# Three value panels of a streaming encoder: products in halves of 256 columns, each activation part used twice in a row, or in row halves of the array into four banks

## The chip, the cores and the metric

The kernel runs on one core of a Trainium2 chip. Its engines are TensorE (PE in the profile, with its weight loads shown apart as PEld), VectorE (DVE), ScalarE (ACT), GpSimd (POOL) and SyncE (SP), which issues the transfers. The metric is the device time in microseconds (us); lower is better. Times of a kernel are medians of several runs.

## The reference, cut to what matters

The reference computes a two-layer encoder trunk over 256 positions and a model width of 2048, all in float32. The change lies in the first mixer, and only in the product that makes its values.

```python
u = rms_norm(h, a_norm_g[l])
proj = u @ a_w_in[l]                      # (256 x 2048) @ (2048 x (3*2048 + 16))
q, k, v, fz = jnp.split(proj, [D, 2 * D, 3 * D], axis=-1)
...
v = v.reshape(B, S, H, Dh)                # 16 heads of 128
...
o = forgetting_attention(q, k, v, logf)
h = h + o.reshape(B, S, D) @ a_w_out[l]
...
```

After it come a squared-ReLU MLP, one shared key and value projection, a second mixer with chunked attention, and a second MLP.

## The kernel before, in words

**Three passes stand for one float32 product.** Every weight tile and every activation is split into a high part, rounded to fp32r, and a low part, the rest. A product is then high x high, low activation x high weight, high activation x low weight. ScalarE makes the high weights (line 210, tile `hi`), VectorE the low ones (line 211, tile `lo`), for a unit of 128 x 1024 weights at a time. `fetch` keeps up to three units ready; `hi` and `lo` have three buffers each, so that the `hi` of a unit needs the buffer of three units before.

**A panel** (`panels`) is 512 output columns. It runs over 8 units of two blocks of 128 rows each (`UA` = 2). In a unit, `products` issues 12 matmuls of 512 columns: two row blocks times two blocks of 128 positions (`NB` = 2) times three passes. `passes` holds the lines of the passes: 444 for high x high, 446 for low activation x high weight, 448 for high activation x low weight. The stationary operand is the activation (128 x 128), the moving one the weights. The sums of a panel stand in a pair of PSUM banks, one for each block of positions, and `acc_pair` deals out two such pairs in turn.

**The order of the work.** The first mixer goes over four groups of four heads. A group has three panels: queries, keys, values. At the end of a key panel, `head_norm` squares the sums, and its last step `turn` (line 529, tile `qn`) reads the bank of each block of positions once more. That step isn't done at once: it goes into a list, `fill`, of which `run_fill` does one entry after each unit. So the key banks of block 0 are read after unit 0 of the value panel, those of block 1 after its unit 1. The attention of a group (`attend`: scores on lines 582 and 583, values times probabilities on lines 614 and 615) is spread in the same way over the units that follow. At the end of a value panel `v_evac` (line 639) scales both banks into SBUF on ScalarE. After the fourth group comes `stage` with the output projection, whose first call runs two panels side by side and takes both pairs of banks.

**The written order holds** on VectorE, ScalarE, TensorE and SyncE: the last line of the kernel fixes it (`keep_order`). Each engine takes its instructions in that order and stands still at the first that has to wait.

Of the kernel before, what the change touches and what calls it, by code (L numbers as in the profile page):

```python
# [9 lines left out]
F32 = mybir.dt.float32  # L10
F32R = mybir.dt.float32r
AF = mybir.ActivationFunctionType
ALU = mybir.AluOpType
AX = mybir.AxisListType

P = 128
T = 256
NB = T // P
D = 2048
KT = D // P  # L20
# [10 lines left out]
UA = UN // 512  # L31
# [16 lines left out]
def trunk(ctx: ExitStack, tc: tile.TileContext, xT, xr, gs, hg, bf, wgate, w_in, w_oa, w1a, w2fa, w2sa,  # L48
          w_kv, w_qb, w_ob, w1b, w2fb, w2sb, rel, out):
    nc = tc.nc  # L50
    V, S, G, TE, SY = nc.vector, nc.scalar, nc.gpsimd, nc.tensor, nc.sync

    def pool(name, bufs, **kw):
        return ctx.enter_context(tc.tile_pool(name=name, bufs=bufs, **kw))
# [6 lines left out]
    wk = pool("wk", 6)  # L61
# [30 lines left out]
    first = sm.tile([P, GH], F32, name="first", bufs=1)  # L92
# [7 lines left out]
    units = deque()  # L100
# [79 lines left out]
    ready = deque()  # L180
# [39 lines left out]
    def fetch(ahead=AHEAD, early=EARLY):  # L220
        while (units or raws) and sum(1 for r in ready if not r[2]) <= ahead and not (half_next() and any(r[2] for r in ready)):
            issue()
        while units and sum(1 for r in raws if r[1]) < early:
            load()
        return ready.popleft()[:2]
# [3 lines left out]
    def run_fill():  # L229
        if fill:  # L230
            for f in fill.popleft():
                f()
# [7 lines left out]
    def acc_pair(which=None):  # L240
        if which is None:
            which, turns[0] = turns[0], 1 - turns[0]
        if which == 2:
            return [ps_s.tile([P, 512], F32, name="s") for _ in range(2)]
        return [ps_acc.tile([P, 512], F32, name="acc", tag=f"acc{which}{b}", bufs=1) for b in range(NB)]
# [37 lines left out]
    def room(tag, name, dtype=F32):  # L283
        return qkv.tile([P, WIDE], dtype, name=name, tag=tag, bufs=1 if tag == "bias" else 2)
# [17 lines left out]
    def steps(make):  # L302
        box = []

        def step():
            if not box:
                box.append(make())
            next(box[0])
        return step
# [24 lines left out]
    def turned(name=None):  # L334
        z = qkv.tile([P, GH * T], F32, name="z")
        return (z, qkv.tile([P, GH * T], F32, name=name, tag=name, bufs=2)) if name else z
# [101 lines left out]
    def passes(items, hi, lo, **kw):  # L438

        def cut(w, j):  # L440
            return w[:, j * 512 : (j + 1) * 512]

        for ps, (xh, _), j, first, _ in items:
            TE.matmul(ps, xh, cut(hi, j), start=first, stop=False, **kw)  # L444
        for ps, (_, xl), j, _, _ in items:
            TE.matmul(ps, xl, cut(hi, j), start=False, stop=False, **kw)  # L446
        for ps, (xh, _), j, _, last in items:
            TE.matmul(ps, xh, cut(lo, j), start=False, stop=last, **kw)  # L448

    def products(ps, hi, lo, x, u, halves=False, fast=None, apart=False):  # L450
        kw = {"skip_group_check": True} if fast else {}

        def item(j, b):
            k = u * UA + j if fast is None or u > 1 else 2 * j + u
            return ps[b], [x[k][:, i, b * P : (b + 1) * P] for i in range(2)], j, k == 0 and not fast, k == KT - 1

        J, B = range(UA), range(NB)
        if apart:
            groups = [[(j, b) for b in B] for j in J]
        elif halves:  # L460
            groups = [[(j, b) for j in J] for b in B]
        else:
            groups = [[(j, b) for b in B for j in J]]
        for g in groups:
            passes([item(*i) for i in g], hi, lo, **kw)
# [10 lines left out]
            items.append((ps[i not in (4, 5)][i in (1, 5)], xp, g % 2, i < 2 and g == 0, i < 2 and g == stop))  # L476
        passes(items, hi, lo, skip_group_check=True)

    def panels(x, evacs, before=None, after=None, which=(None, None), tail=None):
        ps = [acc_pair(i) for i in which[: len(evacs)]]  # L480
        for u in range(KT // UA - (3 if tail else 0)):
            if before:
                before(u)
            for q, evac in enumerate(evacs):
                hi, lo = fetch(min(u // 2, AHEAD), 2) if before else fetch()
                products(ps[q], hi, lo, x, u, not units and not ready, apart=bool(before) and u < 2)
                run_fill()
                if u == KT // UA - 1:
                    for b in range(NB):
                        evac(b, ps[q][b])  # L490
                if after:
                    after()
        if tail:
            tail.x, tail.ps, tail.evac = x, ps, evacs
# [12 lines left out]
    def head_norm(stats, z, dst, late=0, apart=None):  # L507

        rest = []

        def f(b, ps):
            sq = wk.tile([P, 512], F32, name="sq", tag="wk")
            ss = sm.tile([P, GH], F32, name="ss")
            rn = sm.tile([P, GH], F32, name="rn")

            def square():
                S.activation(sq, ps, AF.Square)

            def total():
                V.tensor_reduce(ss, sq.rearrange("p (a d) -> p a d", a=GH), axis=AX.X, op=ALU.add)  # L520

            def norm():
                vv = sm.tile([P, GH], F32, name="vv")
                V.tensor_scalar(vv, ss, 1.0 / P, stats().e[:, b : b + 1], op0=ALU.mult, op1=ALU.add)  # L524
                G.tensor_tensor(rn, vv, mhalf, op=ALU.pow)  # L525

            def turn():
                qn = wk.tile([P, 512], F32, name="qn", tag="wk")
                V.tensor_tensor(qn.rearrange("p (a d) -> p a d", a=GH), ps.rearrange("p (a d) -> p a d", a=GH),
                                rn.unsqueeze(2).to_broadcast([P, GH, P]), op=ALU.mult)  # L530
                blocks32(qn, z, b)

            if apart is None:
                square()
            rest.append((square, total, norm, turn))
            if b == NB - 1:
                turns = [[t] for _, _, _, t in rest] + carry(z, dst)
                if apart is not None:
                    add_fill([[]] * apart + [[s, t, n] for s, t, n, _ in rest] + turns)
                    return  # L540
                for _, total, norm, _ in rest:
                    total()
                    if not late:
                        norm()
                add_fill([[]] * (late - 1) + ([[n for _, _, n, _ in rest]] if late else []) + turns)
        return f

    def scale_q(land, layer, g):
        tag = "qs"[g // 2]
        q = qkv.tile([P, GH, T], F32, name="q", tag=tag, bufs=2)  # L550
        S.activation(q.rearrange("p a (b i c) -> p (a b) i c", b=NB, i=4),
                     land.rearrange("p (i ab c) -> p ab i c", i=4, c=32), AF.Copy, scale=gqk[:, layer : layer + 1])
        return q
# [83 lines left out]
    def v_evac(v, r):  # L637
        def f(b, ps):
            S.activation(v[:, b, :], ps, AF.Copy, scale=r[:, b : b + 1])
        return f  # L640

    def add_fill(items):
        for i, it in enumerate(items):
            if i < len(fill):
                fill[i] = fill[i] + it
            else:
                fill.append(it)


    st0 = RowStats("x")  # L650
    x = []
# [16 lines left out]
    def rows_in(i):  # L668
        b, n = chunks[i]
        c = slice(n * 512, (n + 1) * 512)  # L670
        SY.dma_start(h[b][:, c], xr[b][:, c])
# [86 lines left out]
    for g in range(NG):  # L758
        zq, lq = turned("z")
        qb = {}  # L760
        late = 6 if g == 0 else 0
        panels(x, [head_norm(lambda: st0, zq, lq, late)], begin if g == 0 else None)
        if g == 0:
            step = steps(head_gains)
            add_fill([[step], [], [], [], [step]])
            add_fill([[lambda i=i: rows_in(i)] for i in range(5, 8)])
            add_fill([[lambda i=i: st0.add(*chunks[i])] for i in range(3, 8)])
            fill[4].insert(len(fill[4]), st0.roots)
            add_fill(gates(x, st0))
        add_fill([[]] * (7 + late) + [[lambda qb=qb, lq=lq, g=g: qb.update(q=scale_q(lq, 0, g))]])  # L770
        zk, k = turned(), room("k", "k")[:, : GH * T]
        v = room("v", "v")[:, :UN].rearrange("p (b c) -> p b c", b=NB)
        panels(x, [head_norm(lambda: st0, zk, k)])
        add_fill(attend(g, lambda qb=qb: qb["q"], k, v, lambda: ct["cq"], o, decay_bias))
        panels(x, [v_evac(v, st0.r)])

    def bring(p, name):
        p.t[name] = room("kv"[name in ("12", "21")], "w" + name)
# [146 lines left out]
    for g in range(NG):  # L925
        zk, k = turned(), room("k", "k")[:, : GH * T]
        v = room("v", "v")[:, :UN].rearrange("p (b c) -> p b c", b=NB)
# [85 lines left out]
```

## Time and profile before

| | |
|---|---|
| median of 3 runs | 2124.96 us (2121.89 to 2129.16) |
| span of the profiled execution | 2124.3 us |
| TensorE busy | 2101.3 us (99%), 9278 matmuls |
| weight loads busy | 1729.3 us (81%) |
| VectorE busy | 1654.6 us (78%) |
| ScalarE busy | 1211.3 us (57%) |
| value panels of groups 1, 2, 3 end at | 149.9, 220.6, 291.3 us |

The span goes from the first to the last instruction of one execution; no time of its own is listed for that execution, and the median of the runs lies 0.7 us above its span. The ends of the panels are the starts of the first `v_evac` of each. In the timeline a row is a run of like instructions: start, length of the run, engine, line, operation, tiles, count, and in brackets how long the engine stood idle before it and what ended that. A run of matmuls is longer than the distance to the next one, since one ends after the next has begun.

### The profile page before, as it was taken

Reading aid. Unit: us, or ns where it says so; the run is one execution under the profiler, and the core shown is the slowest. Engines: PE = TensorE matmul, PEld = TensorE weight load, DVE = VectorE, ACT = ScalarE, POOL = GpSimd, SP = SyncE. Lnnn points to the kernel's source line nnn. Section 1 sums busy time; section 2 is a strip of 40 time slices with the busy share of each in tenths; the row PEclk is TensorE's granted clock in tenths of the full one; section 3 lists DMA queues with packets and bytes.
Section 4 is the critical chain, followed back from the end, with each engine's and each line's share of the span. In section 5 each row is a group of like instructions: output and inputs, shape, how many; then the busy total and the mean of one; then the engine's idle time right before and its main releaser. Section 6 shows DMA issues by size and latency. Waiting matters only on the chain.

```text
span 2124.3 us, 26113 instructions
## 1 busy us (share of the span) xinstructions
PE 2101.3 (99%) x9278; PEld 1729.3 (81%) x9278; DVE 1654.6 (78%) x1931; ACT 1211.3 (57%) x1519; POOL 49.1 (2%) x48
## 2 busy tenths in 40 slices
PE   9999999999999999999999999999999999999999
PEld 7888888877888887888788888888788878878887
DVE  5767776888788878878877677678887887888786
ACT  6544445665566566556575454456654655665664
POOL 1001000000000000000001010000000000000000
PEclk9999999999999999999999999999999999999999
DMA  8787788776676576477577777787766766765763
GB/s 281 244 249 243 224 264 255 238 246 210 220 256 206 200 265 228 170 239 269 181 240 261 234 228 235 239 276 237 247 211 217 241 203 222 248 212 195 261 234 129
DMA packets 179283, 491.63 MB, mean 231 GB/s; under 512 B 36416, under 2 KB 73424, under 8 KB 179152
## 3 DMA queue, kind: packets, MB, share of 16 engines
q1 hardware_dynamic: 179152, 489.96, 69.8%
q8 instruction: 73, 1.20, 0.2%
q14 instruction: 58, 0.48, 0.1%
HBM read 450.01 MB, written 39.87 MB: 231 GB/s over the span
## 4 chain that ended last, share of the span: by engine, by line
PE 84%; DVE 7%; DMA 4%; ACT 2%; issue 2%; SPq 1%; ACTq 0%; DVEq 0%
PE acc L446 23%; PE acc L448 23%; PE acc L444 23%; PE s L444 4%; PE s L446 4%; PE s L448 4%; DVE lo L211 3%; ACT hi L210 2%; DVE w L790 1%; DVE loh L211 1%; DMA q<-turn 1%; DMA turn<-z 1%; DMA raw<-in_w_in 1%; DVE wT L790 1%; PE s L583 1%
## 5 line engine op out<-in xcount | busy, mean ns | idle before, releaser
L211 DVE TENSOR_TENSOR lo<-raw,hi 128x1024 fp32r<-128x1024 f32 (+1 forms) x610 | 738.2, 1215 | 260.1 <-ACT hi L210 253.0
L210 ACT ACTIVATE hi<-raw 128x1024 fp32r<-128x1024 f32 (+1 forms) x610 | 640.8, 1053 | 367.3 <-PE acc L446 266.8
L444 PE MATMUL acc<-hi,act 128*128 128x512 f32 x2208 | 608.4, 394 | 2.0 <-ACT hi L210 1.1
L446 PE MATMUL acc<-hi,act 128*128 128x512 f32 x2208 | 599.7, 390 | 6.4 <-DVE act L814 6.4
L448 PE MATMUL acc<-lo,act 128*128 128x512 f32 x2208 | 598.4, 390 | 0.0
L446 PEld LDWEIGHTS acc<-hi,act 128*128 128x128 f32 x2208 | 413.4, 188 | 98.2 <-DVE act L814 10.7
L448 PEld LDWEIGHTS acc<-lo,act 128*128 128x128 f32 x2208 | 413.3, 188 | 89.0 <-DVE lo L211 3.2
L444 PEld LDWEIGHTS acc<-hi,act 128*128 128x128 f32 x2208 | 412.9, 188 | 87.9 <-ACT hi L210 2.1
L210 ACT ACTIVATE hi<-w 128x1024 fp32r<-128x1024 f32 x160 | 169.1, 1057 | 226.4 <-DVE w L790 105.2
L211 DVE TENSOR_TENSOR lo<-w,hi 128x1024 fp32r<-128x1024 f32 x160 | 194.8, 1218 | 83.9 <-ACT hi L210 83.8
L444 PE MATMUL s<-hi,act 128*128 128x512 f32 x416 | 112.6, 389 | 0.0
L446 PE MATMUL s<-hi,act 128*128 128x512 f32 x416 | 112.5, 389 | 0.0
L448 PE MATMUL s<-lo,act 128*128 128x512 f32 x416 | 112.5, 389 | 0.0
L210 ACT ACTIVATE hi<-wT 128x1024 fp32r<-128x1024 f32 x64 | 67.7, 1057 | 54.9 <-DVE wT L790 27.9
L448 PEld LDWEIGHTS s<-lo,act 128*128 128x128 f32 x416 | 78.1, 188 | 16.2
L446 PEld LDWEIGHTS s<-hi,act 128*128 128x128 f32 x416 | 78.1, 188 | 16.2
L444 PEld LDWEIGHTS s<-hi,act 128*128 128x128 f32 x416 | 78.0, 188 | 16.2
L211 DVE TENSOR_TENSOR lo<-wT,hi 128x1024 fp32r<-128x1024 f32 x64 | 78.2, 1222 | 9.4 <-ACT hi L210 7.5
L210 ACT ACTIVATE hih<-w 128x512 fp32r<-128x512 f32 x80 | 49.8, 622 | 24.2 <-PE acc L446 16.0
L617 ACT ACTIVATE act<-po 128x256 fp32r<-128x256 f32 x32 | 12.3, 384 | 86.0 <-PE po L615 86.0
L211 DVE TENSOR_TENSOR loh<-w,hih 128x512 fp32r<-128x512 f32 x80 | 54.8, 685 | 7.3 <-ACT hih L210 7.3
L525 POOL TENSOR_TENSOR rn<-vv,mhalf 128x4 f32<-128x4 f32 x32 | 43.3, 1366 | 385.0 <-DVE vv L524 384.9
(190 smaller groups left out, 1717.0 us busy)
## 6 DMA issues: line engine op xcount, KB each, us to landing
raw<-in_w1a SPq DMA_DIRECT2D x96, 512.0 KB, 4.4
raw<-in_w1b SPq DMA_DIRECT2D x96, 512.0 KB, 4.5
raw<-in_w_in SPq DMA_DIRECT2D x94, 512.0 KB, 4.6
raw<-in_w2sa SPq DMA_DIRECT2D x80, 512.0 KB, 4.3
raw<-in_w2sb SPq DMA_DIRECT2D x80, 512.0 KB, 4.2
raw<-in_w_kv SPq DMA_DIRECT2D x64, 512.0 KB, 4.6
turn<-z SPq DMA_DIRECT2D x60, 512.0 KB, 4.2
w<-in_w2fa SPq DMA_DIRECT2D x32, 768.0 KB, 7.6
```

The lines of the kernel that those rows point to most:

```text
L210: S.activation(hi[:, c], raw[:, c], AF.Copy)
L211: V.tensor_tensor(lo[:, c], raw[:, c], hi[:, c].bitcast(F32), op=ALU.subtract)
L444: TE.matmul(ps, xh, cut(hi, j), start=first, stop=False, **kw)
L446: TE.matmul(ps, xl, cut(hi, j), start=False, stop=False, **kw)
L448: TE.matmul(ps, xh, cut(lo, j), start=False, stop=last, **kw)
L525: G.tensor_tensor(rn, vv, mhalf, op=ALU.pow)
L583: TE.matmul(s[:, P : 3 * P], q[:, a, P:T], k[:, a], start=True, stop=True)
L617: S.activation(o[i][:, 0], po[:, :T], AF.Copy)
L790: V.tensor_tensor(d, a, b, op=op)
```

## The change

The value panels of groups 1, 2 and 3 are given another way of doing units 1 to 6; units 0 and 7 and all other panels stay as they were.

- Group 1, `short_halves`: each matmul of 512 columns becomes two of 256, with the same stationary operand. There are 144 instead of 72.
- Group 2, `repeats`: the three products of a block are issued together: the high activation with high weights, the same high activation with low weights, the low activation with high weights. The number stays 72.
- Group 3, `row_halves`: each matmul over 128 rows becomes two over 64 rows, the lower half and the upper half of the array. The second half adds up in a second pair of banks, which the panel takes with a second call of `acc_pair`. There are 144 of 512 columns. At the end ScalarE copies each bank of the second pair to SBUF, VectorE adds it into the first pair, and `v_evac` follows.

```diff
+    def row_halves(k, b, ps, xs, w, first, last):
+        for i in range(2):
+            c = slice(64 * i, 64 * i + 64)
+            TE.matmul(ps[2 * i + b], xs[c], w[c], start=first and i == 1, stop=last and i == 1, skip_group_check=True)
+
+    def short_halves(k, b, ps, xs, w, first, last):
+        for i in range(2):
+            c = slice(256 * i, 256 * i + 256)
+            TE.matmul(ps[b][:, c], xs, w[:, c], start=False, stop=False, skip_group_check=True)
+
+    def repeats(ps, hi, lo, x, u):
+        for j in range(UA):
+            k, c = u * UA + j, slice(j * 512, (j + 1) * 512)
+            for b in range(NB):
+                xh, xl = (x[k][:, i, b * P : (b + 1) * P] for i in range(2))
+                for xs, w in ((xh, hi), (xh, lo), (xl, hi)):
+                    TE.matmul(ps[b], xs, w[:, c], start=False, stop=False, skip_group_check=True)
+
+    def split_products(how, ps, hi, lo, x, u):
+        if how is repeats:
+            repeats(ps, hi, lo, x, u)
+            return
+        for i, w in ((0, hi), (1, hi), (0, lo)):
+            for j in range(UA):
+                k = u * UA + j
+                for b in range(NB):
+                    how(k, b, ps, x[k][:, i, b * P : (b + 1) * P], w[:, j * 512 : (j + 1) * 512],
+                        k == UA and not i and w is hi, k == KT - UA - 1 and w is lo)
+
...
-    def panels(x, evacs, before=None, after=None, which=(None, None), tail=None):
+    def panels(x, evacs, before=None, after=None, which=(None, None), tail=None, how=None):
         ps = [acc_pair(i) for i in which[: len(evacs)]]
+        if how is row_halves:
+            ps[0] += acc_pair()
...
-                products(ps[q], hi, lo, x, u, not units and not ready, apart=bool(before) and u < 2)
+                if how and 0 < u < KT // UA - 1:
+                    split_products(how, ps[q], hi, lo, x, u)
+                else:
+                    products(ps[q], hi, lo, x, u, not units and not ready, apart=bool(before) and u < 2)
                 run_fill()
                 if u == KT // UA - 1:
                     for b in range(NB):
+                        if how is row_halves:
+                            both = wk.tile([P, 512], F32, name="both", tag="wk")
+                            S.activation(both, ps[q][2 + b], AF.Copy)
+                            V.tensor_tensor(ps[q][b], ps[q][b], both, op=ALU.add)
                         evac(b, ps[q][b])
...
-        panels(x, [v_evac(v, st0.r)])
+        panels(x, [v_evac(v, st0.r)], how=(None, short_halves, repeats, row_halves)[g])
```

## The prediction

> **What bounds the kernel now.** I read the page first, then the timeline of TensorE over the value panel of group 3.
>
> ```profile
> span 2124.3 us, 26113 instructions
> PE 2101.3 (99%) x9278; PEld 1729.3 (81%) x9278; DVE 1654.6 (78%) x1931; ACT 1211.3 (57%) x1519; POOL 49.1 (2%) x48
> ...
> PE 84%; DVE 7%; DMA 4%; ACT 2%; issue 2%; SPq 1%; ACTq 0%; DVEq 0%
> ```
>
> TensorE is idle for 2124.3 - 2101.3 = 23 us, and it makes up 84% of the chain that ends last. There is no slack for it: whatever is added to TensorE in a value panel is added to the time.
>
> ```profile
> 268.38 1.07 PE L444 MATMUL acc<-hi,act 128*128 128x512 f32 x4
> 271.11 0.59 PE L614 MATMUL po<-pbuf,v 128*128 128x256 f32 x2
> 271.54 0.38 PE L615 MATMUL po<-pbuf,v 128*128 128x128 f32 x2
> 271.68 1.17 PE L444 MATMUL acc<-hi,act 128*128 128x512 f32 x4
> 272.68 1.08 PE L446 MATMUL acc<-hi,act 128*128 128x512 f32 x4
> 273.60 1.07 PE L448 MATMUL acc<-lo,act 128*128 128x512 f32 x4
> 274.50 1.07 PE L444 MATMUL acc<-hi,act 128*128 128x512 f32 x4
> ...
> 290.60 1.07 PE L448 MATMUL acc<-lo,act 128*128 128x512 f32 x4
> 291.50 1.07 PE L444 MATMUL acc<-hi,act 128*128 128x512 f32 x4
> ```
>
> Unit 0 (268.38 to 271.11) is 12 matmuls in 2.73 us: 227 ns from one to the next, with no gap anywhere up to the output projection at 291.50. Unit 1 begins at 271.68, unit 2 at 274.50. A matmul lasts about 1.07 - 3 x 0.227 = 0.39 us, so it ends 0.16 us after its successor began.
>
> **Part 1, group 1, halves of 256 columns.** Nothing waits differently: high weights still go first, low weights last. 72 matmuls become 144 with a weight load each. Two things could cost: the load, and what a matmul costs beside its columns.
>
> ```profile
> 111.35 0.59 PE L614 MATMUL po<-pbuf,v 128*128 128x256 f32 x2
> 111.56 0.40 PEld L615 LDWEIGHTS po<-pbuf,v 128*128 128x128 f32 x2
> 111.78 0.38 PE L615 MATMUL po<-pbuf,v 128*128 128x128 f32 x2
> 111.89 0.30 PEld L582 LDWEIGHTS s<-k,q 128*128 128x128 f32 x2
> 112.00 0.39 PE L582 MATMUL s<-k,q 128*128 128x128 f32 x2
> 112.11 0.30 PEld L583 LDWEIGHTS s<-k,q 128*128 128x128 f32 x2
> 112.22 0.60 PE L583 MATMUL s<-k,q 128*128 128x256 f32 x2
> ```
>
> Loads of 128 x 128 follow each other here every 0.11 us (L582 from 111.89 to L583 at 112.11 is two), with a matmul of 0.11 us behind each. So a load does not hold a matmul of half of 227 ns. The second cost shows in a stretch at half clock, quoted under the clock below: there a 512-column matmul takes 0.425 us, which is 213 ns at full clock; 14 ns of the 227 do not follow the clock. If each instruction pays these 14 ns, the panel becomes 72 x 14 ns = 1.0 us longer; if they belong to the columns, nothing; if short matmuls are free of them, 1.0 us (72 x 14 ns) is saved. I take +0.5 us, with -1.0 and +1.0 as ends. A far end is that 256 columns of fp32r run at the pace of the 256-column pass of L614, 0.43 / 2 = 0.215 us each (111.35 to 111.78): 72 x (0.43 - 0.227) = +14.6 us.
>
> **Part 2, group 2, the same part twice in a row.** The count stays. A saving would need the second load to be dropped.
>
> ```profile
> L89 PEld LDWEIGHTS pt<-ones x22: 288/333/338, 1.0 to 5.5; 128*128 128x128 f32 x22
> ```
>
> The warm-up issues 11 matmuls of one and the same stationary tile, and each of their 22 passes has its load. Loads lie behind matmuls anyway, so I price this at 0; the lower end is that 24 dropped loads take their 14 ns with them, -0.3 us. Two waits move: low weights are wanted by the second matmul of a unit, not the ninth, 7 x 0.227 = 1.6 us earlier, and the buffer of high weights comes free 4 x 0.227 = 0.9 us later.
>
> ```profile
> 203.37 1.18 DVE L211 TENSOR_TENSOR lo<-raw,hi 128x1024 fp32r<-128x1024 f32 x1
> 205.82 1.07 ACT L210 ACTIVATE hi<-raw 128x1024 fp32r<-128x1024 f32 x1 [1.66 <-PE acc L446]
> 206.53 1.07 PE L444 MATMUL acc<-hi,act 128*128 128x512 f32 x4
> ```
>
> The low part that ends at 204.55 is for the unit that begins at 206.53, 2.0 us later: the cover stays. The high part at 205.82 is released by TensorE and is for the unit three further on, over 6 us away, so 0.9 us more is hidden. Without that cover the price would be under 1 us.
>
> **Part 3, group 3, halves of the array.** Three costs.
>
> *The pace.* Trace and page of before show no matmul on half the rows. Lower bound: both halves run at once, 227 ns a pair, as now, +0 (or -1.0 us if the 14 ns go). Upper bound: one after the other, 72 x 0.227 = +16.3 us. For the loads two at 0.11 us each just fit in 227 ns. The stationary halves and the banks of a pair are disjoint, nothing in the program orders one after the other; I take +0. The Trainium skill's "TensorE: Matmul & The Clock Gate" (Part 3, packing small matmuls) says that matmuls on different row groups run concurrently and gives 3.07x for four tiles of 32 rows and 512 columns; no run here shows it; an estimate by that figure, 4 / 3.07 = 1.30 for a pack, is 72 x 0.30 x 0.227 = +4.9 us, which would make the sum below 14.4. Entering and leaving the half-array form, twice because the attention's whole-array matmuls stand in between, may let the array run empty: 4 times up to 0.16 us; I take +0.3, ends 0 and 0.65.
>
> *A wait at the start.* The second pair of banks is the one the key panel filled, and `turn` (L529) still reads it.
>
> ```profile
> 272.37 0.42 DVE L618 TENSOR_TENSOR act<-po,act 128x256 fp32r<-128x256 f32 x1 [0.68 <-ACT act L617]
> 272.71 0.68 DVE L529 TENSOR_TENSOR qn<-acc,rn 128x512 f32<-128x512 f32 x1
> 273.43 0.71 DVE L314 STREAM_TRANSPOSE z<-qn 128x512 f32<-128x512 f32 x1
> 274.07 1.18 DVE L211 TENSOR_TENSOR lo<-raw,hi 128x1024 fp32r<-128x1024 f32 x1
> 275.17 0.68 DVE L529 TENSOR_TENSOR qn<-acc,rn 128x512 f32<-128x512 f32 x1
> ```
>
> In the changed program the second matmul of unit 1 waits for VectorE's first `qn` and the fourth for its second. Unit 1 starts at 271.68; the first is done at 273.39, the second at 275.85, behind a transpose and a low part, and VectorE is busy from 272.37 on, so none of it can come earlier. Everything of TensorE is queued behind the fourth matmul: 11 pairs from 275.9 end at 278.4, where unit 2 began at 274.50. Price +3.9 us. Ends: 3.5, and 0 if the wait were already over.
>
> *A wait at the end.* The output projection now begins in the pair that the panel itself filled, since the second call of `acc_pair` shifts the turn.
>
> ```profile
> L639 ACT ACTIVATE v<-acc,rx x8: 672/682/690, 81.0 to 291.8; 128x512 f32<-128x512 f32 x8
> ```
>
> ```profile
> 268.13 1.09 ACT L517 ACTIVATE sq<-acc 128x512 f32<-128x512 f32 x2 [1.07 <-PE acc L448]
> 288.08 1.06 ACT L210 ACTIVATE hi<-raw 128x1024 fp32r<-128x1024 f32 x1 [1.66 <-PE acc L446]
> 291.25 1.27 ACT L639 ACTIVATE v<-acc,rx 128x512 f32<-128x512 f32 x2 [2.11 <-PE acc L448]
> ```
>
> The second pair is complete after unit 6, so ScalarE copies its first bank while it stood idle (289.14 to 291.25): hidden. Then a chain, from 291.25: VectorE adds block 0 (0.68, as `qn`), `v_evac` 0.68, ScalarE's copy of the second bank starting 0.1 early (0.6, half of the two squares' 1.09 and its tail), VectorE adds block 1 (0.68), `v_evac` 0.68, and about 0.04 us from engine to engine. The first two matmuls of the projection can go at 292.7, the third at 294.7; it stood at 291.50 + 0.45 = 291.95. Price +2.75 us; ends 2 and 3.5.
>
> *The clock.* TensorE then does little for a while at two places. The first rows are stretches of before (length, TensorE busy, ..., granted clock), the others matmuls in and behind two of them.
>
> ```profile
> 473.60:477.00 3.40, 1.77 (x8) 1.13 (x6) 1.94 (x3) 2.57 (x4) 0.00 (x0) 1.00 0.36 137
> 1528.30:1531.70 3.40, 1.54 (x8) 0.96 (x7) 3.00 (x4) 3.40 (x5) 0.00 (x0) 1.00 0.05 18
> 1531.73:1535.14 3.41, 3.41 (x10) 2.67 (x9) 3.41 (x5) 1.86 (x3) 0.00 (x0) 0.50 0.49 174
> ```
>
> ```profile
> 477.50 0.70 PE L444 MATMUL s<-hi,Sh 128*128 128x512 f32 x2 [2.13 <-DVE acc L861]
> 1530.68 0.70 PE L444 MATMUL s<-hi,Sh 128*128 128x512 f32 x2 [1.86 <-DVE acc L861]
> 1532.49 0.63 PE L444 MATMUL s<-hih,Sh 128*128 128x512 f32 x1
> 1532.91 0.63 PE L446 MATMUL s<-hih,Sh 128*128 128x512 f32 x1
> 1533.34 0.63 PE L448 MATMUL s<-loh,Sh 128*128 128x512 f32 x1
> ```
>
> After an idle 1.86 us the granted clock was 0.50 for 3.41 us, with 0.425 us from matmul to matmul (1532.49 to 1533.34 is two); after 2.13 us it was not. The stretch of 3.4 us ahead had 1.54 us of matmuls in the first case and 1.77 in the second, so the limit lies near half. One such stretch costs 3.41 x (1 - 227/425) = 1.6 us. The start wait leaves some 0.9 us of matmuls in 4.2 us: half clock nearly always, +1.3 on average, since part of the slow stretch is still waiting. The end wait has 2.4 to 2.7 us idle in 3.2: about every second time, +0.8. Together +2.1, ends 0 and 3.2. The same page of the Trainium skill (Part 1, the clock gate) has the clock fall only after an idle window of about 3.4 us, with no gap over about 3 us as its advice; the trace's 1.86 us disagrees, and the trace decides.
>
> **Sum.** 0.5 + 0 + 0 + 0.3 + 3.9 + 2.75 + 2.1 = 9.55, rounded 9.5 us. The span goes from 2124.3 to 2133.8, and with the 0.7 us that the median of 2124.96 lies above it, the time to 2134.5.
>
> **Rivals.**
> 1. *The halves of the array run one after the other.* No row of before speaks against it. +16.3 on the sum: 25.8, 2150.8 us. Chance 0.22.
> 2. *256 columns fall to the pace of L614.* Against it: fp32r takes 227 ns for 512 where that pass takes 215 for 256, so it is another form. 9.0 + 14.6 = 23.6, 2148.5 us. Chance 0.06.
> 3. *The clock is kept through both waits*: no single gap would be over 2.2 us, and the trace has one of 2.13 us without a drop. 9.5 - 2.1 = 7.4, 2132.4 us. Chance 0.12. The Trainium skill's rule on the clock, told above, is this case.
> 4. *Not slower: the 14 ns go.* If a matmul pays them only because it fills the array with a fresh 128 x 128 x 512 block, all three forms lose them: 3 x 72 x 14 ns = 3.0 us saved. Against 0.3 + 3.9 + 2.75 of waits, and with the clock kept, 3.9 is left: 2128.9 us, no change that can be told. It decides once the waits come to less than 9 us and the saving is whole; if the start wait is over earlier too, it falls to zero. Chance 0.10.
>
> My forecast has 0.50.
>
> **How the numbers follow.** About 0.3% (6.4 us) can be told from no change. Slower: 0.50 + 0.22 + 0.06, and 0.08 of rival 3, which lies just over the bound: 0.86. Same: the other 0.04 and 0.07 of rival 4: 0.11. Faster: 0.03. The range from 2128 to 2153 takes in the ends of the unknown costs of the forecast, rivals 1 to 3 with two us for the spread of the runs, and half of rival 4; some 0.1 is left out.
>
> **What would show it.** In the changed profile: the value panel of group 1 as long as before to 1 us, with 144 matmuls about 0.115 us apart; group 2 unchanged, with as many loads as matmuls; in group 3 pairs of half-array matmuls that start within a few ns and repeat every 227 ns, a wait for `qn` in unit 1 until about 4.2 us after its start, a wait for `v` ahead of the projection, and a granted clock of 0.50 behind the first. Pairs every 454 ns would be rival 1, halves 0.215 us apart rival 2, no wait for `qn` a failure of my largest term.

## The result, and the profile after

The changed kernel takes 2135.97 us (median of 5, 2132.97 to 2137.21) against 2125.29 us: 1.0045 times the time before, 95% interval 1.0031 to 1.0059, or +9.6 us (6.6 to 12.5). (The ratio is not that of the two medians, which lie 10.7 us apart.) Forecast were 2134.5 us and +9.5 us. The profiled execution spans 2133.6 us where 2133.8 was forecast. Below, ratios are given in microseconds by 1% = 21.3 us; line numbers of the changed kernel are 38 higher behind the new functions (`qn` 529 is now 567, values 614 is 652, `v_evac` 639 is 677).

The page after:

```profile
span 2133.6 us, 26410 instructions
PE 2107.5 (99%) x9422; PEld 1735.4 (81%) x9422; DVE 1656.0 (78%) x1933; ACT 1211.8 (57%) x1521; POOL 49.1 (2%) x48
...
PE 85%; DVE 6%; DMA 4%; ACT 2%; issue 2%; SPq 1%; ACTq 0%; DVEq 0%
```

144 matmuls and loads more, TensorE still the bound. Of the 9.3 us in span, TensorE's busy time holds 6.2; the other 3.1 is idle time.

**Group 1.** Units 1 to 6 of its value panel, first row to the first row of unit 7, before and then after (timeline of TensorE):

```profile
130.28 0.47 PE L444 MATMUL acc<-hi,act 128*128 128x512 f32 x1
...
147.38 0.39 PE L444 MATMUL acc<-hi,act 128*128 128x512 f32 x1
```

```profile
130.38 0.48 PE L458 MATMUL acc<-hi,act 128*128 128x256 f32 x2
...
148.37 0.40 PE L444 MATMUL acc<-hi,act 128*128 128x512 f32 x1
```

17.10 us became 17.99: +0.89. The distance from one 256-column matmul to the next is 120 ns for 128 of the 143.

**Group 2.** The instructions of the repeats, shortest, median and longest in ns:

```profile
L466 PEld LDWEIGHTS acc<-hi,act x48: 187/188/192, 202.0 to 218.6; 128*128 128x128 f32 x48
L466 PE MATMUL acc<-hi,act x48: 389/389/474, 202.0 to 218.9; 128*128 128x512 f32 x48
L466 PEld LDWEIGHTS acc<-lo,act x24: 187/188/192, 202.1 to 218.4; 128*128 128x128 f32 x24
L466 PE MATMUL acc<-lo,act x24: 387/389/389, 202.3 to 218.6; 128*128 128x512 f32 x24
```

72 loads for 72 matmuls: none is dropped. The values of groups 1 and 2 are evacuated 70.70 us apart, before and after.

**Group 3, the start.** TensorE, then the two `qn` of VectorE:

```profile
272.12 0.59 PE L652 MATMUL po<-pbuf,v 128*128 128x256 f32 x2
272.55 0.38 PE L653 MATMUL po<-pbuf,v 128*128 128x128 f32 x2
272.86 0.50 PE L453 MATMUL acc<-hi,act 64*128 64x512 f32 x1
274.56 0.50 PE L453 MATMUL acc<-hi,act 64*128 64x512 f32 x2 [1.20 <-DVE qn L567]
277.01 2.57 PE L453 MATMUL acc<-hi,act 64*128 64x512 f32 x13 [1.95 <-DVE qn L567]
```

```profile
273.73 0.68 DVE L567 TENSOR_TENSOR qn<-acc,rn 128x512 f32<-128x512 f32 x1
...
276.18 0.68 DVE L567 TENSOR_TENSOR qn<-acc,rn 128x512 f32<-128x512 f32 x1
```

One matmul goes, the second stands until the first `qn` is done, the fourth until the second is. The third, on the other half and with a bank of its own that was free, doesn't pass the second: both stand in the row at 274.56. The second pair starts at 277.01 instead of 272.86 + 0.23: 3.92 us.

**Group 3, the end.** TensorE from unit 7 on, then ScalarE and VectorE:

```profile
296.01 1.20 PE L444 MATMUL acc<-hi,act 128*128 128x512 f32 x4
...
297.97 1.08 PE L448 MATMUL acc<-lo,act 128*128 128x512 f32 x4
300.18 0.73 PE L444 MATMUL acc<-hi,act 128*128 128x512 f32 x2 [1.13 <-ACT v L677]
302.12 0.79 PE L444 MATMUL acc<-hi,act 128*128 128x512 f32 x1 [1.21 <-ACT v L677]
```

```profile
296.18 0.58 ACT L526 ACTIVATE both<-acc 128x512 f32<-128x512 f32 x1
299.44 0.69 ACT L677 ACTIVATE v<-acc,rx 128x512 f32<-128x512 f32 x1 [2.67 <-DVE acc L527]
300.02 0.59 ACT L526 ACTIVATE both<-acc 128x512 f32<-128x512 f32 x1
301.38 0.69 ACT L677 ACTIVATE v<-acc,rx 128x512 f32<-128x512 f32 x1 [0.77 <-DVE acc L527]
```

```profile
298.70 0.70 DVE L527 TENSOR_TENSOR acc<-acc,both 128x512 f32<-128x512 f32 x1 [0.57 <-PE acc L448]
300.64 0.70 DVE L527 TENSOR_TENSOR acc<-acc,both 128x512 f32<-128x512 f32 x1 [1.24 <-ACT both L526]
```

The chain is the forecast one, link by link: first copy early at 296.18, add, `v_evac`, copy, add, `v_evac`. The third matmul of the projection comes 302.12 - 297.97 = 4.15 us after the last pass began; before it was 291.95 - 290.60 = 1.35. Price 2.80 us.

**The clock**, in two stretches of after (length, busy times of PE, PEld, DVE, ACT, POOL, then the granted clock):

```profile
277.90:281.31 3.41, 3.41 (x20) 3.09 (x18) 0.00 (x0) 1.06 (x1) 0.00 (x0) 0.50 0.77 298
301.79:305.20 3.41, 3.08 (x7) 2.48 (x8) 1.23 (x1) 1.29 (x3) 0.00 (x0) 0.50 0.00 0
```

Both waits were followed by a stretch of half clock, by the estimate of the prediction up to 1.6 us each.

For what follows it helps to have one distance that takes in all of group 3's loss and nothing from elsewhere: from the values ahead of unit 1 (the first `po` row, 271.11 before, 272.12 after) to the first score matmul behind the first unit of the projection (294.23 and 305.94; both rows stand further down). It is 23.12 us before and 33.82 us after. Below it is called the local stretch.

### The profile page after: what moved, and what is told of

It is laid out like the page before. It is cut to its first block, busy times and chain, and to the rows that moved or that the text cites. A ratio compares the mean times of both kernels' runs of the same rounds, so it can differ in the third digit from the quotient of the medians.

```text
span 2133.6 us, 26410 instructions
## 1 busy us (share of the span) xinstructions
PE 2107.5 (99%) x9422; PEld 1735.4 (81%) x9422; DVE 1656.0 (78%) x1933; ACT 1211.8 (57%) x1521; POOL 49.1 (2%) x48
## 4 chain that ended last, share of the span: by engine, by line
PE 85%; DVE 6%; DMA 4%; ACT 2%; issue 2%; SPq 1%; ACTq 0%; DVEq 0%
PE acc L446 22%; PE acc L444 22%; PE acc L448 22%; PE s L444 5%; PE s L446 5%; PE s L448 5%; DVE lo L211 2%; ACT hi L210 2%; DMA raw<-in_w_in 1%; DVE w L828 1%; PE acc L453 1%; PE acc L458 1%; PE acc L466 1%; DVE loh L211 1%; DMA raw<-in_w2sb 1%
## 5 line engine op out<-in xcount | busy, mean ns | idle before, releaser
L444 PE MATMUL acc<-hi,act 128*128 128x512 f32 x2136 | 589.1, 394 | 4.6 <-ACT v L677 2.3
L446 PE MATMUL acc<-hi,act 128*128 128x512 f32 x2136 | 581.5, 391 | 5.3 <-DVE act L852 5.3
L448 PE MATMUL acc<-lo,act 128*128 128x512 f32 x2136 | 579.4, 390 | 0.0
L446 PEld LDWEIGHTS acc<-hi,act 128*128 128x128 f32 x2136 | 400.2, 188 | 94.9 <-DVE act L852 10.2
L444 PEld LDWEIGHTS acc<-hi,act 128*128 128x128 f32 x2136 | 399.4, 188 | 89.3 <-ACT v L677 3.2
L448 PEld LDWEIGHTS acc<-lo,act 128*128 128x128 f32 x2136 | 400.1, 188 | 86.5 <-DVE lo L211 2.9
L656 DVE TENSOR_TENSOR act<-po,act 128x256 fp32r<-128x256 f32 x32 | 13.6, 425 | 49.9 <-ACT act L655 49.9
```

The costliest lines, as they stand in the source:

```text
L656: V.tensor_tensor(o[i][:, 1], po[:, :T], o[i][:, 0].bitcast(F32), op=ALU.subtract)
```

## The experiments

Theory: the loss is group 3's, and there it is two waits for PSUM banks and the clock behind them; half-array matmuls as such run two at a time at no cost. Rivals: the short matmuls cost; the half-array form itself costs.

**One panel alone.** Only `how` is changed:

```diff
-        panels(x, [v_evac(v, st0.r)], how=(None, short_halves, repeats, row_halves)[g])
+        panels(x, [v_evac(v, st0.r)], how=(None, None, None, row_halves)[g])
```

> Only the value panel of group 3 is changed (halves of the array); groups 1 and 2 stay as before. Theory (waits): the changed kernel's trace puts 0.9 us on group 1, nothing on group 2 and 10.7 us on group 3, of which 3.9 is the wait for the key banks at the start, 3.0 the wait for the evacuation at the end, about 3 two stretches of half clock and 0.8 the changes of form. So +9.5 to +10.7 us here, hardly less than the whole change. Rival (short matmuls): if the loss lay in groups 1 and 2, it would be gone here, +2 us or less.

Measured: 1.0046 (1.0032 to 1.0061), +9.8 us. Its local stretch is 32.22 us; the clock fell behind the start wait alone. And with `(None, short_halves, repeats, None)`:

> Only groups 1 and 2 are changed (halves of 256 columns, the same part twice in a row); group 3 stays as before. Theory: +0.9 us from the 72 added instructions at 13 ns each, 0 from the repeats; no change that can be told. Rival (short matmuls): +8 us or more.

Measured: 1.0010 (1.0001 to 1.0018), +2.1 us (0.2 to 3.8). The short matmuls as the main cause are out.

**Other banks for the second half.**

```diff
-            ps[0] += acc_pair()
+            ps[0] += acc_pair(2)
```

> As the changed kernel in all three panels, but the second pair of banks of the row halves comes from the score pool, which no other work uses in that panel, so that neither the key banks nor the order of the pairs afterwards is touched. Theory (waits): start wait, end wait and both stretches of half clock go; left are 0.9 us of group 1 and 0.8 of changes of form, +1.7 us, and pairs of half-array matmuls still every 227 ns. Rival (the form itself): if the half-array form is what costs, by its pace or by its changes of form, this stays at +8 us or more.

Measured: 1.0004 (0.9993 to 1.0015), +0.9 us. Nearly all of the loss is gone with the same matmuls. Its timeline, from the values ahead of unit 1 to the first matmul of the projection:

```profile
274.34 0.59 PE L652 MATMUL po<-pbuf,v 128*128 128x256 f32 x2
...
275.08 0.49 PE L453 MATMUL acc<-hi,act 64*128 64x512 f32 x1
275.09 0.49 PE L453 MATMUL s<-hi,act 64*128 64x512 f32 x1
275.42 0.39 PE L453 MATMUL acc<-hi,act 64*128 64x512 f32 x1
275.42 0.39 PE L453 MATMUL s<-hi,act 64*128 64x512 f32 x1
...
292.72 1.20 PE L444 MATMUL acc<-hi,act 128*128 128x512 f32 x4
...
295.60 1.07 PE L444 MATMUL acc<-hi,act 128*128 128x512 f32 x4
```

The two halves of a pair start together, and no wait is left. From the values to the projection it takes 21.26 us; before, 271.11 to 291.50 was 20.39. So the changes of form cost 0.87 us: the first pair is followed after 0.34 us, the values come 0.74 us ahead of it where they came 0.57 ahead of unit 1, and so on at the other three places.

**The end wait alone.** The same spare banks, and the turn of the pairs shifted, so that the projection begins in the panel's own pair:

```diff
-            ps[0] += acc_pair()
+            ps[0] += acc_pair(2)
+            turns[0] = 1 - turns[0]
```

> As the run with the spare banks, but the turn of the bank pairs is shifted, so that the output projection begins in the pair that the value panel filled. It puts back the end wait alone. Theory (waits): +1.7 and the end wait of 2.95, and a stretch of half clock of up to 1.6: +4.7 to +6.3 us. Rival (the form itself): the same time as with the spare banks.

Measured: 1.0017 (1.0008 to 1.0026), +3.6 us (1.7 to 5.5). Between the run with spare banks and the changed kernel, as the theory has it, though a good microsecond under its forecast. The shortfall isn't in group 3: the local stretch is 28.37 us, 4.39 more than the 23.98 with the spare banks, which is the end wait of 2.80 and 1.6 of half clock. The wait is there, with the half clock behind it:

```profile
293.99 0.73 PE L444 MATMUL acc<-hi,act 128*128 128x512 f32 x2 [1.13 <-ACT v L678]
295.94 1.22 PE L444 MATMUL acc<-hi,act 128*128 128x512 f32 x2 [1.21 <-ACT v L678]
```

```profile
295.70:299.10 3.40, 3.16 (x8) 2.49 (x9) 1.23 (x1) 1.28 (x3) 0.00 (x0) 0.50 0.02 5
```

**The start wait filled.**

```diff
+        if how is row_halves and u == 1:
+            busy = ps_o.tile([P, 512], F32, name="pt", tag="po")
+            for _ in range(15):
+                TE.matmul(busy, x[2][:, 0, :P], hi[:, :512], start=True, stop=True)
```

> The changed kernel with 15 added matmuls of 512 columns into a spare bank ahead of unit 1 of the row halves; their sums are read by nobody. They fill 15 x 0.227 = 3.4 us of the 4.1 us that TensorE waits there for the key banks. Theory (the clock follows idle time): no time is lost by them, the stretch of half clock behind the start wait goes, and the time is 1.6 us below the changed kernel, about +8 to +9 us over the kernel before. Rival (the clock falls by the change to half arrays, or at random): the half clock stays, and the time with it, or 3.4 us are added if the wait isn't there to be filled.

Measured: 1.0038 (1.0024 to 1.0051), +8.1 us; that interval alone does not part it from the changed kernel. The trace does:

```profile
273.26 3.67 PE L475 MATMUL pt<-hi,act 128*128 128x512 f32 x15
276.86 2.55 PE L453 MATMUL acc<-hi,act 64*128 64x512 f32 x16
```

```profile
273.00:281.00 8.00, 8.00 (x52) 6.66 (x52) 4.89 (x8) 2.39 (x3) 1.14 (x1) 1.00 0.82 264
```

Fifteen useless matmuls fit into the wait, the clock stays at 1.00, and from the values of group 2 to those of group 3 it takes 76.21 us in place of 77.87: 1.66 us less, for more work. In this trace the clock didn't fall behind the end wait either. So its local stretch shows the two waits without the clock: 30.75 us, 7.63 over before, where 0.87 + 3.92 + 2.80 = 7.59. The 3.07 us that the changed kernel takes beyond it are the two stretches of half clock. The drop behind the start wait is idle time's doing.

**Why the same wait drops the clock in one run and not in another.** In the clock record of all fourteen traces, two drops always lie a whole number of 3.413 us apart (in the trace after, 20.48 us or 6 of full clock between the first two, then 184.32 or 54). So the clock is decided on a fixed grid of 3.413 us that doesn't begin anew with a wait. Leaving out the first 30 us and the last 10 us of each trace there are 20 drops, and each follows a stretch of the grid in which TensorE was busy for 1.60 us or less; no stretch with 1.65 us or more was followed by one. The end wait of the changed kernel lay for the most part in one such stretch (first row); that of the run with group 3 alone was cut in two by the grid (the other rows), and the clock was kept:

```profile
298.37:301.79 3.42, 1.41 (x5) 0.51 (x4) 1.40 (x2) 1.59 (x3) 0.00 (x0) 1.00 0.47 161
```

```profile
294.36:297.77 3.41, 2.28 (x10) 1.32 (x8) 1.60 (x4) 1.18 (x2) 0.00 (x0) 1.00 0.57 183
297.77:301.18 3.41, 2.20 (x10) 1.76 (x10) 1.71 (x2) 1.99 (x3) 0.00 (x0) 1.00 0.02 7
```

**All of one half first.** With the spare banks, `split_products` runs over the half outside the passes:

```diff
+        halves = range(2) if how is row_halves else [None]
-        for i, w in ((0, hi), (1, hi), (0, lo)):
+        for half, i, w in [(half, i, w) for half in halves for i, w in ((0, hi), (1, hi), (0, lo))]:
...
```

What is left out hands `half` on to `row_halves`, which then issues that half alone.

> As the run with the spare banks, but in each unit the 12 matmuls of the lower half come first and the 12 of the upper half after them, instead of in turns. Theory (only neighbours on different halves run at once): each unit has 22 steps of 0.227 us instead of 12, 6 x 10 x 0.227 = 13.6 us more than with the spare banks, about +15 us over the kernel before. Rival (half-array matmuls take half the time whatever their order, or the array finds the other half by itself): the time of the run with the spare banks.

Measured: 1.0045 (1.0031 to 1.0059), +9.6 us. Units 1 to 6 take 26.32 us (271.80 to 298.12), 8.68 over the 17.64 (275.08 to 292.72) with the spare banks. Neither theory: 13.6 was a miss, and no change is out too. The seam between two units (`s` is the upper half of the old unit, `acc` the lower half of the next):

```profile
279.63 0.39 PE L453 MATMUL s<-lo,act 64*128 64x512 f32 x1
279.63 0.49 PE L453 MATMUL acc<-hi,act 64*128 64x512 f32 x1
279.85 0.39 PE L453 MATMUL s<-lo,act 64*128 64x512 f32 x1
279.97 0.39 PE L453 MATMUL acc<-hi,act 64*128 64x512 f32 x1
280.08 0.39 PE L453 MATMUL s<-lo,act 64*128 64x512 f32 x1
...
280.31 0.39 PE L453 MATMUL s<-lo,act 64*128 64x512 f32 x1
```

All `s` rows stand ahead of the `acc` rows in the program. Yet the first `acc` starts while three `s` still wait. So more overlaps than direct neighbours: 12 + 8.68 / (6 x 0.227) = 18.4 steps for a unit instead of 22. To test that, the half inside the passes, in fours:

> As the run with the spare banks, but four matmuls of the lower half come first, then the four of the upper half for the same pass, and so on. In the run with whole units one half after the other, a matmul began while three earlier ones of the other half still waited. Theory (TensorE looks past three waiting matmuls of the other half): fours run side by side as well as turns, 12 steps of 0.227 us for a unit, the time of the run with the spare banks, about +1 to +2 us over the kernel before. Rival (only direct neighbours run at once): 18 steps for a unit, 6 x 6 x 0.227 = 8.2 us more.

Measured: 1.0001 (0.9992 to 1.0010), +0.2 us. Units 1 to 6 take 18.11 us (272.19 to 290.30): 0.47 more than in turns, where direct neighbours alone would have cost 8.2. TensorE looks past three matmuls that wait for the other half of the array. It doesn't look past one that waits for a bank: in the changed kernel the third matmul of unit 1 stood behind the second.

**The short form everywhere.** `how=short_halves` for eleven panels:

> All eleven panels of the first mixer after the first one take their units 1 to 6 in halves of 256 columns; no repeats and no row halves. Theory (a fixed 13 ns for each matmul): 11 x 0.9 = +9.8 us, with 120 ns from one 256-column matmul to the next. Rival (loads or covers): where the attention's work lies beside, the doubled loads or later buffers open waits, +15 us or more; rival (columns): no change.

Measured: 1.0040 (1.0027 to 1.0054), +8.5 us. The three panels of a group take 73.43 us in place of 70.70, 0.91 each, and matmuls are 120 ns apart: the fixed cost of a matmul, with no new wait. `how=repeats` for the same eleven:

> All eleven panels of the first mixer after the first one issue the three products of a block together, the same high activation twice in a row; nothing else is changed. Theory (no load is dropped, and the moved waits are covered by 2 us or more): no change, within 1.5 us, with as many loads as matmuls. Rival (cover): in panels beside softmax work the low weights come too late for the second matmul, +3 us or more. Rival (dropped loads): 11 x 0.3 = -3.5 us.

Measured: 1.0011 (1.0000 to 1.0023), +2.3 us (0.0 to 4.9), more than the 1.5 us of its forecast. Its trace doesn't show them in the panels: groups 2 and 3 take 70.70 us, as before to the hundredth, and the score matmul behind the projection's first unit stands at 293.98 (294.23 before). So the repeats cost nothing and save nothing there, and where the 2.3 us come from stays open; TensorE waited twice for low weights, 0.9 us in all, so the cover is thin once or twice in eleven panels.

**How short a matmul may be.** In group 1 alone, four quarters:

```diff
-        for i in range(2):
-            c = slice(256 * i, 256 * i + 256)
+        for i in range(4):
+            c = slice(128 * i, 128 * i + 128)
```

> Only the value panel of group 1 is changed: units 1 to 6 in four matmuls of 128 columns in place of one of 512, 288 in place of 72. Theory (a fixed 13 ns for each matmul and nothing else): 0.067 us each, 0.27 for four, 72 x 0.04 = +2.9 us. Rival (the load of the stationary operand, 0.11 us from one to the next, becomes the bound): 0.44 us for four, 72 x 0.21 = +15 us. Rival (fp32r under 256 columns goes at another pace): more than that.

Measured: 1.0063 (1.0049 to 1.0077), +13.4 us. Units 1 to 6:

```profile
128.87 0.31 PE L458 MATMUL acc<-hi,act 128*128 128x128 f32 x1
...
161.72 0.44 PE L444 MATMUL acc<-hi,act 128*128 128x512 f32 x1
```

32.85 us, +15.75: 0.445 us for four. The fixed 13 ns alone are refuted. Two cuts into unlike parts, `slice(0, 384), slice(384, 512)` and `slice(0, 320), slice(320, 512)`, were to part the load from a slow pace:

> Only the value panel of group 1 is changed: units 1 to 6 in two matmuls of 384 and 128 columns in place of one of 512. With four quarters of 128 columns matmuls and loads both stood 0.112 us apart, which either the load or a slow pace of narrow fp32r matmuls would give. Theory (the load is the bound): here two loads take 0.224 us and hide behind 0.173 + 0.067 = 0.240 us of matmuls; as with two halves, +0.9 us in the panel. Rival (128 columns of fp32r go at two cycles a column, 0.112 us whatever the load): 0.173 + 0.112 = 0.285 us, 72 x 0.058 = +4.2 us in the panel.

> Only the value panel of group 1 is changed: units 1 to 6 in two matmuls of 320 and 192 columns in place of one of 512. Theory (the load is the bound): 0.147 + 0.093 = 0.240 us for the two, +0.9 us in the panel. Rival (fp32r under 256 columns goes at two cycles a column): 0.147 + 0.165 = 0.312 us, 72 x 0.085 = +6.1 us in the panel. If 384 and 128 are slow and these are not, the bound of the slow pace lies between 128 and 192 columns.

Measured: 1.0017 (1.0008 to 1.0027), +3.6 us, and 1.0016 (1.0006 to 1.0027), +3.4 us. Units 1 to 6 of each:

```profile
129.75 0.42 PE L457 MATMUL acc<-hi,act 128*128 128x384 f32 x1
...
151.08 0.44 PE L444 MATMUL acc<-hi,act 128*128 128x512 f32 x1
```

```profile
129.50 0.39 PE L457 MATMUL acc<-hi,act 128*128 128x320 f32 x1
...
148.84 0.42 PE L444 MATMUL acc<-hi,act 128*128 128x512 f32 x1
```

21.33 and 19.34 us: 0.227 + 4.23 / 72 = 0.286 us for the first pair, 0.227 + 2.24 / 72 = 0.258 us for the second. Loads that hide behind a pair (0.240 both times) are refuted by the first, the slow pace (0.312) by the second, and a slow pace that starts between 128 and 192 columns (0.240 for the second) too. What fits all three is a third reading, formed after these runs: only the load of the next matmul runs ahead, so each matmul holds the array for at least one load, 0.111 us. Then four quarters take 4 x 0.111 = 0.444, the others 0.173 + 0.111 = 0.284 and 0.147 + 0.111 = 0.258. The load rows of the two traces fit it: a load begins 2 to 5 ns behind the start of the 128-column or 192-column matmul ahead of it, never earlier, and loads stand in turn 109 and 178 ns apart with 384 + 128 columns, 109 and 150 with 320 + 192. No run was made to refute this reading in its turn: none has a short matmul without a load of its own, so the load isn't parted from a least time of 0.111 us that any matmul might have.

## Why the prediction was right

| term | forecast, us | measured, us | from |
|---|---|---|---|
| group 1, 256 columns | +0.5 (-1.0 to +1.0) | +0.89 | trace after |
| group 2, repeats | 0 | 0.00 | trace after |
| pace of the pairs | 0 (to +16.3) | 0 | spare banks |
| changes of form | +0.3 (0 to 0.65) | +0.87 | spare banks |
| start wait | +3.9 | +3.92 | trace after |
| end wait | +2.75 | +2.80 | trace after |
| clock | +2.1 (0 to 3.2) | +3.1 | trace after, against the filled wait |
| sum | 9.55 | 11.6 | |

- The first term sat between three mechanisms. The upper one holds: each instruction pays its 13 ns (2 x 120 - 227), 72 more pay 0.89 to 0.96. The reading that gave the 14 ns was loose, though: a cost that doesn't follow the clock would stand in the slow stretch too, as 2 x 213 + 14 = 440 ns from matmul to matmul, and that stretch has 425. The 13 ns show at full clock alone.
- The two waits, the largest terms, hold to 0.05 us. They came from who reads a bank last and from the order of the pairs, not from any duration of a matmul.
- The changes of form are the mis-sized term: +0.3 was taken, up to 0.16 us of overhang at each of four places, and the 0.87 lies over even the upper end of 0.65; it is about 0.22 each.
- The clock fell behind both waits in this trace. Over the traces with a wait left open it fell behind the start wait in 2 of 2 and behind the end wait in 2 of 4, which makes 2.4 us on average where 2.1 stood. The runs themselves say the same: the granted clock of the five runs after is 0.9976 on average, that of 80 runs of the kernel before 0.9989, and this is 1.6 stretches of half clock more, some 2.5 us. The limit near half of the prediction is confirmed and narrowed (1.60 us busy of 3.41 drops, 1.65 doesn't); what it lacked is the fixed grid. Where the Trainium skill ("TensorE: Matmul & The Clock Gate", Part 1) asks for an idle window of about 3.4 us, these drops came after gaps of 1.20 and 1.95 us: the measurement decides against it.
- The Trainium skill's rule of concurrent row groups (same page, Part 3) is confirmed for two halves in fp32r: with the spare banks they start within 0.01 us, a pair every 0.227 us. The prediction's estimate by the Trainium skill's figure, 1.30 for a pack of four, does not hold for these two.
- Rival 1 (one half after the other) and rival 2 (the slow pace of 256 columns) are refuted by the spare banks and by 120 ns in group 1. Rival 3 (clock kept) is refuted in the trace after, where the clock fell behind both waits. Rival 4 (the 14 ns go) is refuted: they stay in all three forms.

The terms of group 3 (0.87 + 3.92 + 2.80 + 3.1 = 10.7) account for the local stretch, which grew by 10.70 us. Here is its end, the first matmul of the attention behind the start of the projection, before and then after:

```profile
294.23 0.38 PE L582 MATMUL s<-k,q 128*128 128x128 f32 x2
```

```profile
305.94 0.38 PE L620 MATMUL s<-k,q 128*128 128x128 f32 x2
```

It stands 11.71 us later, of which 0.56 us were there before the first changed panel (values of group 0 at 81.52 instead of 80.96). The span is only 9.3 us longer: from there to the end the changed kernel took 2.4 us less, in code that the change leaves alone. From this matmul to the end the fourteen traces took 1825.7 to 1833.2 us, with no order by kernel. So the closeness of the forecast to the median is in part chance: the sum of the changed panels is 11.6 us where both half clocks fall, the smaller misses all lie on one side, and the spread of the rest is a few us either way. What makes that spread was not tried. The clock is a small part of it: runs of the kernel before with a granted clock of 1.000 took 2125.3 us on average (16 runs), with 0.999 2126.5 (39), with 0.998 2127.2 (23), and within one value they lie 6 to 12 us apart.

## What to carry to other kernels

Where TensorE is the bound, ask of every PSUM bank that a change takes: who reads it last, and how far down that engine's queue does the read stand? The changed matmuls themselves cost under 1 us a panel; borrowing two banks cost 7 us in waits and 2 to 3 us in clock, and banks that nobody used gave nearly all of it back. Half-array matmuls bring no speed where whole ones fit; if they must be, use turns or fours of the two halves and separate banks, and keep an fp32r matmul with its own load at 256 columns or more.

## What the runs showed of the hardware that was not expected

- A matmul with its own 128 x 128 load holds the array for at least 0.111 us: quarters of 128 columns double the panel's time (17.10 to 32.85 us for units 1 to 6), and 384 + 128 columns take 0.286 us, not 0.240. The reading that only one load runs ahead fits these three runs; it was formed after them.
- Matmuls on the two halves of the array start out of the program's order: one began past three waiting matmuls of the other half, and fours of each half ran nearly as fast as turns (18.11 and 17.64 us for units 1 to 6). A matmul that waits for a bank holds up those of the other half too (274.56).
- The clock falls to 0.50 for 3.41 us behind a stretch of a fixed grid of 3.413 us in which TensorE was busy for 1.60 us or less (20 of 20 drops; none at 1.65 or more), also where single matmuls stand in between. A wait with 2.3 us idle in all left the clock alone where the grid cut it in two; fifteen useless matmuls in a wait kept the clock at 1.00.
